# RWKV core of a four-layer backbone: triangular blocks of 16 instead of 32, joined by small TensorE products

## The chip, the cores and the metric

One Trainium2 chip, one of its cores. The metric is the device time of one execution in microseconds (us). Three runs of the kernel before took 2153.38 to 2157.12 us, median 2154.14 us. A fourth execution was profiled, and all rows below come from it.

## The reference, cut to what matters

Four layers (retention, mLSTM, RWKV-7, retention) over 256 context tokens and 256 latents of width 1024. Only the token mixing of layer 2 is touched. For each of 16 heads of width 64, in both directions, it runs

```
def step(S, inp):
    rt, wt, kt, vt, at, bt = inp
    sa = jnp.einsum('bhij,bhj->bhi', S, at)
    S = S * wt[:, :, None, :] + sa[..., None] * bt[:, :, None, :] + vt[..., None] * kt[:, :, None, :]
    return S, jnp.einsum('bhij,bhj->bhi', S, rt)
```

The term with `sa` makes each step depend on the one before. In a chunk of 64 steps it becomes a unit triangular matrix of 64 x 64 for each head, which has to be inverted before the chunk's outputs and its new state are plain matrix products.

## The kernel before

The core (`rk_core`) works in 8 batches, n = 0 to 7. Batch n holds chunks 2(n//2) and 2(n//2)+1 of both directions for one half of the heads (n%2): 4 units of 4 head pairs. The stages of a batch are

- P (`prep`, twice, one for each direction): loads, decay, scan on VectorE (L1294), the scaled operands W (L1301, L1308), bb (`bdA`, L1306) and kb (L1318, GpSimd).
- G (`grams1`, four times): 192-column products (L1328). Their triangles go to `AD` (four copies of 32 rows on ScalarE), the 32 x 32 part that lies off the diagonal goes to `off`, the rest to `RB`.
- H (`grams2`, four times): products for `AK` (L1344).
- I (`solve`): 32 x 32 triangles. `AD` is masked (L1366) and turned by a VectorE transpose in blocks of 32 into `LS` (L1367), so that each partition holds whole triangles. Then 30 steps run, each a product and an addition (L1378, L1379): the first 6 columns on GpSimd, in a copy that ScalarE makes, the others on VectorE. GpSimd's columns are copied back (L1381), the diagonal is set (L1382), and two transposes (L1384, L1385) give `O1` and `O2`.
- J (`whole`): two diagonal 32 x 32 blocks of each head and the block below become the 64 x 64 inverse `M`. Four ScalarE copies bring the diagonal blocks over, 16 products (L1396) make Q, which is copied, 16 products (L1403) make the lower block, which is copied. Then L1409 multiplies `M` by `RB`, which gives `G`.
- T (`step`, four times): L1424, L1426, L1433, L1435, L1436 and the state's update (L1439), with a state S for each direction and half.

ScalarE makes most copies, since `ENG[3]` sets `vcopy = copy`; `qcopy` and `gcopy` stay on VectorE.

Buffers tie the stages together. There are four W tiles, two in each batch, so P of batch n+2 writes what T of batch n read last. There is one `LS` and one `M`, two `AD`, and two PSUM banks under the tag `ps`, which whole, finish and others share.

The order written out is `ORDER`: in round n, P, G, H, I, J of batch n, and then T of batch n-1. What runs on an engine is not that order alone: the program is built with `schedule_with_timeline_sim=True`, and a planner lays each engine's instructions out by its own estimates. So instructions of other stages stand between the steps of a solve.

Batch 0 runs beside the last projections of the layer. The opening of the pools of the other batches (`second`) follows in the program behind them. Batch 7 is followed by `finish`, the output projection and the normalisation. Pieces of layer 3's modulation (`ada`, L308) are put beside batches 6 and 7.

Of the kernel before, what the change touches and what calls it, by code (L numbers as in the profile page):

```python
# [7 lines left out]
F32 = mybir.dt.float32  # L8
# [4 lines left out]
OP = mybir.AluOpType  # L13
# [18 lines left out]
SC = 6  # L32
# [100 lines left out]
class Net:  # L133
# [830 lines left out]
    def rwkv(self, i, j):  # L964
        nc, a = self.nc, self.a
        mm = nc.tensor.matmul
        with ExitStack() as es:
            prk = self.pool(es, "rk", 1)
            c = lambda name, *shape: prk.tile([128, *shape], F32, name=name)
            K = {}  # L970
            consts = (("mix", (6, 8)), ("kk", (8,)), ("hsel", (2,)), ("hb32", (128,)), ("w2", (1024,)), ("a2", (1024,)), ("ka", (8,)),
                      ("w0", (2, 8)), ("a0", (2, 8)), ("rk", (8,)), ("gng", (8,)), ("gnb", (8,)), ("II", (64,)), ("mak", (2, 128)),
                      ("mrb", (2, 64)), ("mtri", (32,)), ("reset", (512,)))
# [211 lines left out]
    def rk_core(self, es, e0, K, B, xd, h, xx, p1, p0):  # L1185
        nc = self.nc
# [57 lines left out]
        small = [t.rearrange("p (q h t) -> p q h t", q=4, h=2) for t in few[:8]]  # L1244
        roff = Ring(small, zero)
# [78 lines left out]
        def grams1(u, b0, AD):  # L1324
            d, W = u["d"], u["W"]
            g = two()
            for p in range(4):
                mm(g[:, p, 0:192], cat(u["bb"][:, p]), W[:, p], start=True, stop=True)  # L1328
            off = u["off"] = roff.next()
            for q in range(4):  # L1330
                r, half = slice(32 * q, 32 * q + 32), q % 2
                (vcopy if half else copy)(AD[r, :, b0:b0 + 4].rearrange("p t q -> p q t"), g[r, :, 32 * half:32 * half + 32])
            for h in range(2):
                r = slice(64 * h, 64 * h + 32)
                copy(off[r, :, h], g[r, :, 32:64])
# [25 lines left out]
        def solve(n, AD):  # L1361

            LS, O2 = [pool[tag] if tag in pool else pool.setdefault(tag, block(tag)) for tag in ("LS", "O2")]
            fl = lambda t: t.rearrange("p a b -> p (a b)")
            o = AD[:, :, 0:16]
            nc.vector.tensor_tensor(out=o, in0=o, in1=K["mtri"].unsqueeze(2).broadcast_to([128, 32, 16]), op=OP.mult)  # L1366
            nc.vector.transpose(fl(LS), fl(AD))  # L1367
            if SC:
                copy(fl(AD), fl(LS))
            for s in range(1, 31):  # L1370
                m = 31 - s

                for eng, A, lo, hi in ((nc.gpsimd, AD, 0, min(s, SC)), (nc.vector, LS, SC, s)):
                    if hi > lo:
                        n = hi - lo
                        t = p0.tile([128, SC * (31 - SC) if A is AD else (31 - SC) ** 2 // 4], F32, tag="sol" + "p" * (A is AD), bufs=1, name="sol")
                        t = t[:, 0:m * n].rearrange("p (a b) -> p a b", b=n)
                        eng.tensor_tensor(out=t, in0=A[:, s + 1:, s:s + 1].broadcast_to([128, m, n]), in1=A[:, s:s + 1, lo:hi].broadcast_to([128, m, n]), op=OP.mult)  # L1378
                        eng.tensor_tensor(out=A[:, s + 1:, lo:hi], in0=A[:, s + 1:, lo:hi], in1=t, op=OP.add)  # L1379
            if SC:  # L1380
                nc.gpsimd.tensor_copy(LS[:, :, 0:SC], AD[:, :, 0:SC])  # L1381
            nc.vector.memset(fl(LS)[:, ::33], 1.0)  # L1382
            O1 = AD
            nc.vector.transpose(fl(O1), fl(LS))  # L1384
            nc.vector.transpose(O2, LS.rearrange("p t s -> p s t"))  # L1385
            return O1, O2

        def whole(units, O1, O2):

            for q in range(4):  # L1390
                r, half = slice(32 * q, 32 * q + 32), q % 2
                (vcopy if half else copy)(M[r, :, q // 2, 32 * half:32 * half + 32], O2[r, :, 0:16].rearrange("p t q -> p q t"))
            Q = pool["Q"]
            qp = bank("ps").rearrange("p q t -> p (q t)")[0:64].rearrange("p (q t) -> p q t", q=16)
            for b in range(16):
                mm(qp[:, b], cat(units[b // 4]["off"][:, b % 4]), O2[:, :, b], start=True, stop=True)  # L1396
            for h in range(2):
                (qcopy if h else copy)(Q[64 * h + 32:64 * h + 64, :, h], qp[32 * h:32 * h + 32])
            for x in range(2):
                bs = slice(8 * x, 8 * x + 8)  # L1400
                tp = bank("ps").rearrange("p q t -> p (q t)")[0:32].rearrange("p (q h t) -> p q h t", q=8, h=2)
                for b in range(8):
                    mm(cat(tp[:, b]), O1[:, :, 8 * x + b], cat(Q[:, 8 * x + b]), start=True, stop=True)  # L1403
                for h in range(2):
                    (qcopy if h else copy)(M[64 * h + 32:64 * h + 64, bs, h, 0:32], tp[:, :, h])
# [142 lines left out]
        def second():  # L1548
# [4 lines left out]
            for nm in ("fin", "Y", "G", "mu", "rs", "bc"):  # L1553
                pool[nm] = p2
# [7 lines left out]
            pool["Q"] = p2.tile([128, 16, 2, 32], F32, name="Q")  # L1562
            zero(pool["Q"])
# [26 lines left out]
def host(inp):  # L1590
# [71 lines left out]
    a["rk_mtri"] = one(s % 32 < np.arange(32)[None, :])  # L1662
# [18 lines left out]
```

## Time and profile before

| what | value |
|---|---|
| median of 3 runs | 2154.14 us |
| profiled execution, time | 2151.38 us |
| its span, first to last instruction | 2149.6 us |
| core's batches, first transpose (L1367) of batch 0 to the last G copy of batch 7 | about 1225 to 1714 us of the span |
| mean granted TensorE clock | 0.957 |

A row of a timeline gives the start in us from the span's begin, the duration, the engine, line, operation, what is written and read, and how many instructions are merged. A float32 product shows as two records on PE and two on PEld. `ps`, `g` and `pp` are PSUM tiles, and some buffers go by the name of an earlier tile at their place: `bdB` is also `M`, `O` is `O2`, `q` and `lnsq` are `off`.

### The profile page before, as it was taken

How to read it: one execution, taken by the hardware profiler on the slowest of the kernel's cores; microseconds unless marked ns; L12 is line 12 of the kernel's file. 1: busy time of each engine (PE TensorE's matmuls, PEld its weight loads, DVE VectorE, ACT ScalarE, POOL GpSimd, SP SyncE). 2: the span in 40 equal slices, each digit the busy share in tenths (PEclk: the TensorE clock that was granted, in tenths of full speed). 3: DMA queues.
4: the chain of work that ended last, by engine and by line, in shares of the span. 5: the costliest groups of instructions: out<-in, count | busy, mean ns of one | idle time of the engine just before them, and what ended most of it. 6: DMA issues, size and time to landing. Idle time of an engine off the chain costs nothing. (4 is left out here: it accounts for less than half of the span.)

```text
span 2149.6 us, 35145 instructions
## 1 busy us (share of the span) xinstructions
PE 1947.1 (91%) x13562; PEld 1654.9 (77%) x13562; DVE 1344.2 (63%) x2456; ACT 941.9 (44%) x1851; POOL 612.7 (29%) x940
## 2 busy tenths in 40 slices
PE   7999999999999989989899987778778988999996
PEld 5788888877777777776658976677777776999995
DVE  4463635457646377576877467888776776665554
ACT  3242424233435454343445555556576352444433
POOL 1000000006200244322503257666555432311001
PEclk9999999999999989989899998999888999999998
DMA  9333324332545454343234411102123750233331
GB/s 303 109 108 114 122 90 134 106 108 75 196 168 178 148 174 153 112 130 109 99 115 161 150 55 54 35 23 66 32 74 94 224 173 1 79 118 118 118 103 46
DMA packets 241527, 245.94 MB, mean 114 GB/s; under 512 B 30992, under 2 KB 200080, under 8 KB 241360
## 3 DMA queue, kind: packets, MB, share of 16 engines
q1 hardware_dynamic: 241360, 243.70, 36.3%
q8 instruction: 107, 1.75, 0.3%
q14 instruction: 60, 0.49, 0.1%
HBM read 216.26 MB, written 27.39 MB: 113 GB/s over the span
## 5 line engine op out<-in xcount | busy, mean ns | idle before, releaser
L240 DVE TENSOR_TENSOR wl<-wraw,wh 128x1024 fp32r<-128x1024 f32 x216 | 270.5, 1254 | 192.1 <-ACT wh L238 187.3
L238 ACT ACTIVATE wh<-wraw 128x1024 fp32r<-128x1024 f32 x216 | 228.5, 1059 | 263.5 <-PE pp L257 119.3
L256 PE MATMUL pp<-hA,wh 128*128 128x512 f32 (+1 forms) x704 | 255.3, 365 | 7.1 <-DVE rp L527 3.0
L257 PE MATMUL pp<-hB,wh 128*128 128x512 f32 (+1 forms) x704 | 254.9, 363 | 0.0
L258 PE MATMUL pp<-hA,wl 128*128 128x512 f32 (+1 forms) x704 | 254.6, 363 | 0.1
L256 PE MATMUL pp<-zh,wh 128*128 128x512 f32 (+1 forms) x620 | 215.4, 350 | 10.1 <-ACT zh L288 6.0
L258 PE MATMUL pp<-zh,wl 128*128 128x512 f32 (+1 forms) x620 | 210.4, 340 | 0.0
L257 PE MATMUL pp<-zl,wh 128*128 128x256 f32 (+1 forms) x512 | 168.7, 330 | 3.0 <-DVE zl L289 3.0
L367 DVE SCALAR_TENSOR_TENSOR x<-pp,mod,x 128x256 f32<-128x256 f32 x192 | 87.3, 480 | 131.1 <-PE pp L258 130.8
L256 PEld LDWEIGHTS pp<-hA,wh 128*128 128x128 f32 x704 | 132.5, 189 | 32.0 <-PE pp L258 3.6
L258 PEld LDWEIGHTS pp<-hA,wl 128*128 128x128 f32 x704 | 133.1, 189 | 24.1 <-issue 1.6
L257 PEld LDWEIGHTS pp<-hB,wh 128*128 128x128 f32 x704 | 133.1, 189 | 22.4 <-issue 1.7
L256 PE MATMUL pp<-wh,hA 128*128 128x256 f32 x512 | 146.7, 288 | 2.0 <-ACT wh L238 1.9
L256 PEld LDWEIGHTS pp<-zh,wh 128*128 128x128 f32 x620 | 117.7, 191 | 37.9 <-issue 10.3
L257 PE MATMUL pp<-wl,hA 128*128 128x256 f32 x512 | 145.6, 285 | 0.5 <-DVE wl L240 0.5
L258 PE MATMUL pp<-wh,hB 128*128 128x256 f32 x512 | 145.3, 284 | 0.0
L258 PEld LDWEIGHTS pp<-zh,wl 128*128 128x128 f32 x620 | 117.8, 190 | 19.1 <-issue 6.7
L1378 POOL TENSOR_TENSOR sol<-AD 128x84 f32<-128x84 f32 (+13 forms) x240 | 94.7, 394 | 104.3 <-ACT AD L1198 86.5
L257 PEld LDWEIGHTS pp<-zl,wh 128*128 128x128 f32 x512 | 97.7, 191 | 16.7 <-issue 5.4
L1379 POOL TENSOR_TENSOR AD<-AD,sol 128x84 f32<-128x84 f32 (+13 forms) x240 | 101.8, 424 | 18.1
L256 PEld LDWEIGHTS pp<-wh,hA 128*128 128x128 f32 x512 | 97.7, 191 | 5.9 <-issue 2.6
L257 PEld LDWEIGHTS pp<-wl,hA 128*128 128x128 f32 x512 | 97.9, 191 | 1.4 <-DVE wl L240 0.8
(520 smaller groups left out, 4878.3 us busy)
## 6 DMA issues: line engine op xcount, KB each, us to landing
wraw<-ret_w_in SPq DMA_DIRECT2D x96, 512.0 KB, 3.7
wraw<-ada_w SPq DMA_DIRECT2D x56, 512.0 KB, 4.1
wraw<-ret_w_out SPq DMA_DIRECT2D x32, 512.0 KB, 3.4
wraw<-ml_w_in SPq DMA_DIRECT2D x32, 512.0 KB, 3.8
wraw<-rk_w_rkvg SPq DMA_DIRECT2D x32, 512.0 KB, 3.7
adaw<-ada_w SPq DMA_DIRECT2D x48, 256.0 KB, 4.6
raw<-ada_w SPq DMA_DIRECT2D x16, 512.0 KB, 7.8
wraw<-ml_w_out SPq DMA_DIRECT2D x16, 512.0 KB, 4.7
```

The costliest lines, as they stand in the source:

```text
L238: nc.scalar.activation(h, t, ACT.Copy)
L240: (nc.gpsimd if self.nsplit % 4 in self.psplit else nc.vector).tensor_tensor(out=l, in0=t, in1=f(h), op=OP.subtract)
L256: mm(ps, lhs[0], rhs[0], start=start, stop=False)
L257: mm(ps, lhs[0], rhs[1], start=False, stop=False)
L258: mm(ps, lhs[1], rhs[0], start=False, stop=stop)
L367: self.nc.vector.scalar_tensor_tensor(out=x, in0=ps, scalar=self.gate(i, c, st), in1=x, op0=OP.mult, op1=OP.add)
L1378: eng.tensor_tensor(out=t, in0=A[:, s + 1:, s:s + 1].broadcast_to([128, m, n]), in1=A[:, s:s + 1, lo:hi].broadcast_to([128, m, n]), op=OP. ...
L1379: eng.tensor_tensor(out=A[:, s + 1:, lo:hi], in0=A[:, s + 1:, lo:hi], in1=t, op=OP.add)
```

## The change

Blocks of 16 are inverted on VectorE alone: both diagonal 16 x 16 blocks of a triangle lie in one access pattern (`k`), 14 steps instead of 30. GpSimd has no part in the recursion. It cuts out the 16 x 16 blocks below the diagonal (`los`) first. Two rounds of 32 x 32 products, four at a time at the four diagonal positions of the array, join the blocks to inverses of 32 (`M`'s diagonal), a third gives their transposes (`MT`), and two rounds at two positions join 32 to 64.

```diff
-            LS, O2 = [pool[tag] if tag in pool else pool.setdefault(tag, block(tag)) for tag in ("LS", "O2")]
+            LS = p0.tile([128, 1056], F32, tag="LS", bufs=1, name="LS")
+            for b0 in (0, 8):
+                t = rLo.next()
+                nc.gpsimd.tensor_tensor(out=t, in0=AD[:, :, b0:b0 + 8], in1=K["m16"][:, 1].unsqueeze(2).broadcast_to([128, 32, 8]), op=OP.mult)
+                los.append(t)
             o = AD[:, :, 0:16]
-            nc.vector.transpose(fl(LS), fl(AD))
-            if SC:
-                copy(fl(AD), fl(LS))
-            for s in range(1, 31):
-                m = 31 - s
-                for eng, A, lo, hi in ((nc.gpsimd, AD, 0, min(s, SC)), (nc.vector, LS, SC, s)):
-                    ...
-            if SC:
-                nc.gpsimd.tensor_copy(LS[:, :, 0:SC], AD[:, :, 0:SC])
+            nc.vector.transpose(flat, fl(AD))
+            A = LS.rearrange("p (k x) -> p k x", x=528)[:, :, 0:512].rearrange("p k (a b) -> p k a b", b=32)
+            for s in range(1, 15):
+                m = 15 - s
+                t = p0.tile([128, 112], F32, tag="sol", bufs=1, name="sol")[:, 0:2 * m * s].rearrange("p (k a b) -> p k a b", k=2, b=s)
+                nc.vector.tensor_tensor(out=t, in0=A[:, :, s + 1:16, s:s + 1].broadcast_to([128, 2, m, s]), in1=A[:, :, s:s + 1, 0:s].broadcast_to([128, 2, m, s]), op=OP.mult)
+                nc.vector.tensor_tensor(out=A[:, :, s + 1:16, 0:s], in0=A[:, :, s + 1:16, 0:s], in1=t, op=OP.add)
...
+            ps, Pm = wide(), part("Pm")
             for b in range(16):
-                mm(qp[:, b], cat(units[b // 4]["off"][:, b % 4]), O2[:, :, b], start=True, stop=True)
...
+                for o, r in quarters:
+                    mm(ps[r, b], los[b // 8][r, :, b % 8], O2[r, :, b], start=True, stop=True, tile_position=(o, o))
+            nc.vector.tensor_tensor(out=Pm, in0=ps, in1=K["m16"][:, 2].unsqueeze(1).broadcast_to([128, 16, 32]), op=OP.add)
+            ps, MT = wide(), part("MT")
+            for b in range(16):
+                for o, r in quarters:
+                    mm(ps[r, b], O1[r, :, b], Pm[r, b], start=True, stop=True, tile_position=(o, o))
+            for q, (o, r) in enumerate(quarters):
+                (vcopy if q % 2 else copy)(M[r, :, q // 2, 32 * (q % 2):32 * (q % 2) + 32], ps[r])
+            ps = wide()
+            for b in range(16):
+                for o, r in quarters:
+                    mm(ps[r, b], Pm[r, b], O1[r, :, b], start=True, stop=True, tile_position=(o, o))
+            copy(MT, ps)
+            ps, Q = wide(), part("Pm")
...
+                    mm(ps[r2, b], units[b // 4]["off"][r, b % 4], M[r, b, h, 0:32], start=True, stop=True, tile_position=(o, o2))
+            for h, (o, r, o2, r2) in enumerate(low):
+                (qcopy if h else copy)(Q[r2], ps[r2])
...
+                    mm(ps[r2, b], MT[r2, b], Q[r2, b], start=True, stop=True, tile_position=(o2, o2))
+            for h, (o, r, o2, r2) in enumerate(low):
+                (qcopy if h else copy)(M[r2, :, h, 0:32], ps[r2])
```

Besides: `off` loses its zeroed half and takes half a small tile, `los` takes the other small tiles (`rLo`), the mask `mtri` becomes `m16` (three masks, 96 columns instead of 32), and the pool tile Q of 1024 columns goes for `Pm` and `MT` of 512 each.

## Rows read from the trace of the kernel before

**Rows 1.** The page, parts 1 and 2: busy shares, and tenths in 40 slices.
```profile
PE 1947.1 (91%) x13562; PEld 1654.9 (77%) x13562; DVE 1344.2 (63%) x2456; ACT 941.9 (44%) x1851; POOL 612.7 (29%) x940
...
POOL 1000000006200244322503257666555432311001
PEclk9999999999999989989899998999888999999998
```
**Rows 2.** Windows: busy us of each engine, clock, DMA; batch 0, 2 to 6, 7.
```profile
1224.00:1260.00 36.00, 36.00 (x180) 29.68 (x179) 30.64 (x62) 11.20 (x26) 24.24 (x61) 1.00 0.16 52
1345.00:1662.00 317.00, 251.10 (x2051) 228.63 (x2052) 247.36 (x496) 189.22 (x448) 190.96 (x372) 0.90 0.19 54
1662.00:1714.00 52.00, 47.98 (x634) 38.33 (x633) 38.28 (x101) 17.41 (x34) 23.45 (x66) 1.00 0.67 212
```
**Rows 3.** Groups by line, 1224 to 1714 us: count, busy us, mean ns, idle before.
```profile
L1379 POOL TENSOR_TENSOR AD<-AD,sol 128x84 f32<-128x84 f32 (+13 forms) x240 | 101.8, 424 | 18.1
L1378 POOL TENSOR_TENSOR sol<-AD 128x84 f32<-128x84 f32 (+13 forms) x240 | 94.7, 394 | 104.3 <-ACT AD L1198 86.5
L1379 DVE TENSOR_TENSOR LS<-LS,sol 128x24 f32<-128x24 f32 (+5 forms) x192 | 74.9, 390 | 6.7 <-ACT AD L1198 1.9
L1378 DVE TENSOR_TENSOR sol<-LS 128x24 f32<-128x24 f32 (+5 forms) x192 | 70.9, 369 | 4.7
...
L1358 DVE TENSOR_TENSOR AK<-g,cmak 128x512 f32<-128x512 f32 x32 | 21.7, 678 | 2.8 <-PE g L1344 1.5 <-ACT bon L1198 1.1
...
L1198 ACT ACTIVATE G<-ps 128x512 f32<-128x512 f32 x16 | 9.6, 601 | 9.4 <-PE ps L1409 9.4
```
**Rows 4.** Timeline: first and later links of the loop from batch 2 to 4.
```profile
1298.39 1.25 DVE L1367 STREAM_TRANSPOSE LS<-AD 128x1024 f32<-128x1024 f32 x1
...
1448.40 0.39 PE L1435 MATMUL pp<-S,W 128*128 128x128 f32 x2
...
1470.41 1.23 DVE L1367 STREAM_TRANSPOSE LS<-AD 128x1024 f32<-128x1024 f32 x1
...
1521.03 1.88 DVE L1385 STREAM_TRANSPOSE O<-LS 128x1024 f32<-128x1024 f32 x1
...
1539.93 2.05 PE L1409 MATMUL ps<-RB,bdB 128*128 128x128 f32 x16
...
1584.00 0.39 PE L1436 MATMUL pp<-bdB,G 128*128 128x128 f32 x2
```
**Rows 5.** Timeline of batch 7, from the solve's first transpose to L1409.
```profile
1663.17 1.24 DVE L1367 STREAM_TRANSPOSE LS<-AD 128x1024 f32<-128x1024 f32 x1
...
1697.02 1.92 DVE L1385 STREAM_TRANSPOSE O<-LS 128x1024 f32<-128x1024 f32 x1
...
1698.97 4.38 ACT L1198 ACTIVATE bdB<-O 32x512 f32<-32x512 f32 x4 [2.43 <-DVE O L1385]
...
1703.38 0.59 ACT L1198 ACTIVATE Q<-ps 32x512 f32<-32x512 f32 x1
...
1704.00 0.69 DVE L1199 COPY Q<-ps 32x512 f32<-32x512 f32 x1 [4.49 <-ACT Q L1198]
...
1704.83 1.94 PE L1403 MATMUL ps<-Q,AD 128*32 128x64 f32 x31 [0.95 <-DVE Q L1199]
...
1707.63 0.97 PEld L1409 LDWEIGHTS ps<-RB,bdB 128*128 128x128 f32 x8 [0.20 <-issue]
```
**Rows 6.** Groups by line and form, VectorE, 1428 to 1439 us.
```profile
L1378 DVE TENSOR_TENSOR sol<-LS 128x84 f32<-128x84 f32 x1 | 0.3, 319 | 0.0
...
L1379 DVE TENSOR_TENSOR LS<-LS,sol 128x84 f32<-128x84 f32 x1 | 0.2, 247 | 0.0
```
**Rows 7.** Groups by line and form, GpSimd, whole span.
```profile
L528 POOL TENSOR_TENSOR rp<-rp,rp 128x256 f32<-128x256 f32 x32 | 30.3, 948 | 194.7 <-DVE rp L527 194.6
```
**Rows 8.** Timeline, PE: four column tiles at once, and single products.
```profile
28.41 0.65 PE L308 MATMUL ps<-raw,csil 128*32 128x64 f32 x32 [0.64 <-DMA raw<-ada_w]
...
1698.99 1.13 PE L1396 MATMUL ps<-O,q 128*64 128x32 f32 x16 [1.31 <-DVE O L1385]
1699.95 1.11 PE L1396 MATMUL ps<-O,lnsq 128*64 128x32 f32 x16
```

More of the change, by code (lines that the diff above doesn't have):

```diff
@@ L31 @@
 ENG = (0, 0, 1, 1, 1, 0, 0, 0)
-SC = 6
 EARLY, FIN = 0, 3
@@ L1243, in rk_core @@
         zero(M)
-        small = [t.rearrange("p (q h t) -> p q h t", q=4, h=2) for t in few[:8]]
-        roff = Ring(small, zero)
+        roff = Ring([t[:, k:k + 128].rearrange("p (q t) -> p q t", q=4) for t in few[:4] for k in (0, 128)])
+        rLo = Ring([t.rearrange("p (t b) -> p t b", b=8) for t in few[4:8]])
         rW = Ring([p1.tile([128, 4, 2, 192], F32, tag=f"W{m}", bufs=1, name=f"W{m}") for m in range(2)], lambda t: nc.gpsimd.tensor_copy(
@@ L1334, in grams1 @@
                 r = slice(64 * h, 64 * h + 32)
-                copy(off[r, :, h], g[r, :, 32:64])
+                copy(off[r], g[r, :, 32:64])
             t = u["RB"] = rRB.next()
@@ L1361, in solve @@
         def solve(n, AD):
-            LS, O2 = [pool[tag] if tag in pool else pool.setdefault(tag, block(tag)) for tag in ("LS", "O2")]
+            LS = p0.tile([128, 1056], F32, tag="LS", bufs=1, name="LS")
+            O2 = pool["O2"] if "O2" in pool else pool.setdefault("O2", block("O2"))
             fl = lambda t: t.rearrange("p a b -> p (a b)")
-            o = AD[:, :, 0:16]
-            nc.vector.tensor_tensor(out=o, in0=o, in1=K["mtri"].unsqueeze(2).broadcast_to([128, 32, 16]), op=OP.mult)
@@ L1367, in solve @@
-            nc.vector.transpose(fl(LS), fl(AD))
-            if SC:
-                copy(fl(AD), fl(LS))
-            for s in range(1, 31):
-                m = 31 - s
-                for eng, A, lo, hi in ((nc.gpsimd, AD, 0, min(s, SC)), (nc.vector, LS, SC, s)):
[L1374 to L1379, printed above, removed]
@@ L1380, in solve @@
-            if SC:
-                nc.gpsimd.tensor_copy(LS[:, :, 0:SC], AD[:, :, 0:SC])
-            nc.vector.memset(fl(LS)[:, ::33], 1.0)
-            O1 = AD
[L1384 to L1394, printed above, removed]
-            for b in range(16):
-                mm(qp[:, b], cat(units[b // 4]["off"][:, b % 4]), O2[:, :, b], start=True, stop=True)
[L1397 to L1405, printed above, removed]
@@ new lines, in solve @@
+            for s in range(1, 15):
[3 more added lines that the diff above has]
+                nc.vector.tensor_tensor(out=A[:, :, s + 1:16, 0:s], in0=A[:, :, s + 1:16, 0:s], in1=t, op=OP.add)
+            nc.vector.memset(flat[:, ::33], 1.0)
@@ new lines, in solve, with whole @@
+            O1 = AD
+            nc.vector.transpose(fl(O1), flat)
+            nc.vector.transpose(O2, flat.rearrange("p (t s) -> p s t", t=32))
+            return O1, O2, los
+        def whole(units, O1, O2, los):
+            quarters = [(32 * q, slice(32 * q, 32 * q + 32)) for q in range(4)]
+            part = lambda name: tl(name, 1, 16, 32)
+            wide = lambda: bank("ps").rearrange("p q t -> p (q t)").rearrange("p (b t) -> p b t", t=32)
+            ps, Pm = wide(), part("Pm")
+            for b in range(16):
+                for o, r in quarters:
[13 more added lines that the diff above has]
+            ps, Q = wide(), part("Pm")
+            low = [(64 * h, slice(64 * h, 64 * h + 32), 64 * h + 32, slice(64 * h + 32, 64 * h + 64)) for h in range(2)]
+            for b in range(16):
+                for h, (o, r, o2, r2) in enumerate(low):
+                    mm(ps[r2, b], units[b // 4]["off"][r, b % 4], M[r, b, h, 0:32], start=True, stop=True, tile_position=(o, o2))
+            for h, (o, r, o2, r2) in enumerate(low):
+                (qcopy if h else copy)(Q[r2], ps[r2])
+            ps = wide()
+            for b in range(16):
+                for o, r, o2, r2 in low:
+                    mm(ps[r2, b], MT[r2, b], Q[r2, b], start=True, stop=True, tile_position=(o2, o2))
+            for h, (o, r, o2, r2) in enumerate(low):
+                (qcopy if h else copy)(M[r2, :, h, 0:32], ps[r2])
@@ L1552, in second @@
             p2 = self.pool(es, "c2", 1, side="right")
-            for nm in ("fin", "Y", "G", "mu", "rs", "bc"):
+            for nm in ("fin", "Y", "G", "mu", "rs", "bc", "Pm", "MT"):
                 pool[nm] = p2
@@ L1661, in host @@
     a["rk_mrb"] = c(one(np.stack([s <= t, 63 - s >= t], 1)))
-    a["rk_mtri"] = one(s % 32 < np.arange(32)[None, :])
+    s, t = (p % 32)[:, None], np.arange(32)[None, :]
+    a["rk_m16"] = c(one(np.stack([(s < t) & (s // 16 == t // 16), s // 16 < t // 16, s == t], 1)))
     r = np.ones((128, 512), np.float32)
```

7 lines of the change are left out of this document (4 added, 3 removed).

## The prediction

> **What bounds the kernel now.** I read the page first. PE is busy 91% of the span, yet in the slices of the RWKV core POOL's digit rises to 6 and the clock's falls to 8 [rows 1], so the core is another regime than the projections around it. The windows come next. In batches 2 to 6 PE is busy 251 of 317 us (79%) at a clock of 0.90, VectorE 247 (78%), POOL 191 (60%), ScalarE 189 (60%) [rows 2]: no engine is full, so latency and queues set the pace. The groups show who fills two engines: the recursion of solve, 480 instructions on POOL (196.5 us) and 384 on VectorE (145.8 us) [rows 3], that is 24.6 and 18.2 us in each of 8 batches. Last I read the timeline for the loop that sets the pace.
>
> The first transpose of the solve starts at 1298.39 us in batch 1 and at 1663.17 in batch 7 [rows 4, 5], 364.8 us for 6 batches: 60.8 us each. The loop reaches over two batches, because T of batch n frees the W tiles that P of batch n+2 writes. From batch 2 to 4 [rows 4]: last read of W at 1448.8, the transpose of batch 4's triangles at 1470.4 (21.6 us for P and G), the last transpose ends at 1522.9 (solve, 52.5), the first L1409 at 1539.9 (whole, 17.0), T ends at 1584.4 (44.5). The sum is 135.6 us for two batches. The largest link is the solve. Where little else is queued it takes 1663.17 to 1698.94, that is 35.8 us, and whole then takes 8.7 us, up to 1707.63 [rows 5]. The other 16.7 us of batch 4's solve are instructions of other stages that the planner put between its steps.
>
> **The change, part by part.** *Solve.* The POOL recursion goes, and with it the ScalarE copy and POOL's copy back. VectorE does 28 instructions instead of 48. Their sizes are 2s(15-s) for s = 1 to 14, 1120 elements in all, 80 on average. The nearest form is that of 84 elements: 319 and 247 ns at a time when few others ran [rows 6], mean 283. 28 x 0.283 = 7.9 us, and with 35 ns between two of them 8.9. The patterns have one dimension more, which no row shows: between 6 us (as the shortest quarter of the present ones) and 10.6 us (28 x 0.38, the present mean with POOL beside it [rows 3]); I keep 8.9. POOL's new part is two masks of 128 x 256. Such an instruction averages 0.95 us [rows 7]. The first reads units 0 and 1, which are there earlier, so one stands on the path, ahead of the VectorE mask that overwrites AD: +0.95. With the three transposes (1.24, about 1.25, 1.92 [rows 5]), the memset and hand-overs (0.3) the new solve takes 0.95 + 1.24 + 8.9 + 1.25 + 1.92 + 0.3 = 14.6 us instead of 35.8: -21.2 on the path.
>
> *Whole.* Two rounds of products become five: three of 64 (128 PE records each) and two of 32 (64 records). The price of a record is the unknown. Singly, 16 records of L1396 start within 0.96 us (1698.99 to 1699.95), 60 ns each, with a tail of 0.17 [rows 8]. Four column tiles at once: 32 records in 0.65 us, less that tail 15 ns each [rows 8]. No row has four row and column positions together. The ends are 7 ns (half as many columns as that row) and 60 ns. I take 15, the row that also runs four at a time, and 30 for the two-position rounds. That is 5 x 1.9 = 9.6 us of PE for each batch, where 64 x 60 ns = 3.8 go: +5.8.
>
> The Trainium skill has a rule against this: TensorE: Matmul & The Clock Gate, section "Wait — 56ns, not 53.3ns?", says that with one decode setting the sequencer spends about 62 ns on each matmul. By it 256 products would take 15.9 us, an estimate from that page, and the forecast would be some 35 us later. The row disagrees: 16 products (32 records) ran in 0.65 us, at most 41 ns each [rows 8].
>
> Between the rounds stand the addition that makes Pm (VectorE from PSUM, as AK, 0.68 [rows 3]), ScalarE's copies of M's diagonal (four at 0.59, the price of Q's copy [rows 5], three of which the next round needs, 1.8 us, covered by the third round), MT's copy (0.60, as G's [rows 3], covered by the fourth round), Q's copies and the last copies (0.69 each, ScalarE and VectorE side by side). The path is 9.6 + 0.68 + 0.69 + 0.69 + 6 hand-overs of 0.2 = 12.9 us instead of 8.7: +4.2. The four M copies of 4.38 us that read O2 strided [rows 5] go. ScalarE comes out lighter by some 2.5 us in a batch, which no path needs.
>
> *The rest has one answer.* A wider mask constant is loaded during the projections, small memsets go, `off` is half as large, and the pool tiles are as large as before: nothing, all of it ahead of batch 1 or on idle engines. SP gets no DMA more in the core.
>
> *What else moves.* VectorE per batch: 47.4 us now (247.4 x 60.8/317), minus 18.2 plus 7.9 plus 0.7: 38. POOL: 36.6 minus 24.6 plus 1.9: 14. PE: 48.2, of which at full clock some 43.4 would be left (x 0.90); plus 5.8 makes 49.2 us. So PE is late next: it sets a floor of about 49 us for a batch. New waits come on PE's queue: a round that waits for Pm or Q holds whatever is queued behind it, mostly products of T and G. Who waits for those is R's copies and the state's update.
>
> *Sum.* The loop over two batches: solve 52.5 becomes 14.6 plus as large a share of others' work as now (16.7 x 14.6/35.8 = 6.8), so -31; whole 17.0 becomes 12.9 plus five hops at about 2 us (two hops cost 8.3 beyond the 8.7 now; ScalarE and VectorE are less full), so +6. That is -25, or 48 us for a batch if only the loop counted. Loop and PE both lie near 49, and two limits so near each other cost beyond either; I take 53. Batches 1 to 7: 6 x (60.8 - 53) = 47. The tail from batch 7's solve: -21.2 + 4.2 = -17; DMA is at 0.67 and PE at 92% there with the next layer's modulation [rows 2], so I count half, -9. Batch 0: PE is full until the projections end (36.00 of 36.00 [rows 2]), its solve is covered, its longer whole is not: +4. Total -52: from the profiled execution's 2151.4 to 2099.5. The median lies 2.8 us above that execution: 2102.
>
> **The rivals.** *Deeper.* PE's tails overlap in the denser stream and the clock goes to full, T runs faster too: 47 us a batch, 6 x 13.8 = 83, the tail whole at 18: 2053. For it: PE's 48.2 includes time at half clock. Against: nothing has shown the core that dense.
>
> *Hops eat it.* Each of the five hops costs 4.1 us, as the two of batch 4 do (17.0 against 8.7), and the planner keeps 16.7 us of others' work inside the solve. Whole 33 (+16), solve 31 (-22): -6 for two batches, -18 in all, tail -5, batch 0 +4: 2135. For it: both are what batch 4 shows. Against: the queues get shorter.
>
> *Slower: the small tiles do not run together.* All products of a round write one PSUM bank from four row positions. If they went singly, 512 x 60 ns = 30.7 us in a batch, PE needs 43.4 - 3.8 + 30.7 = 70 us, above the present 60.8: 6 x 9.5 = +57, tail +3, batch 0 +15: 2229. It decides from 41 ns a record (43.4 - 3.8 + 512 x 0.041 = 60.8). The Trainium skill has this as a rule (TensorEngine Tiling (Array Packing), Restrictions and Gotchas, Gotcha 1): different row tiles cannot access one PSUM bank at the same time. No row here shows row tiles in one bank. Against it stands the 15 ns row, with column tiles alone in one bank.
>
> *No effect.* T or the planner's order holds the loop whatever the solve does: 2154.
>
> **How the numbers follow.** Forecast 0.48 (its own range 2080 to 2122), deeper 0.14, hops 0.21, singly 0.11, no effect 0.06. The range leaves out the singly and part of the deepest and the no-effect cases: 2046 to 2143. Faster by over 0.2% (4.3 us, about what a measurement of this kernel can tell from no change): forecast, deeper and nearly all of hops, 0.82; within 0.2%: 0.06; slower: singly and a little more, 0.12.
>
> **What would show it.** The recursion's 28 VectorE instructions near 0.28 us and a solve of 15 to 22 us from first to last transpose; the 64-product rounds at about 1.9 us, under 1 or near 8 would tell another price; transposes L1367's counterpart about 53 us apart; PE's windows over 90% busy with a clock above 0.90; POOL under 25% in the core. It would be wrong if whole takes over 30 us, if PE is still under 80% busy at a period near 60, or if the rounds go singly.

## The result

The changed kernel took 2124.29 us (median of 4 runs, 2119.65 to 2128.6), the kernel before 2153.76 in the runs beside it: a ratio of 0.9865, 95% interval 0.9849 to 0.988. The profiled execution took 2119.65 us with a span of 2117.9 (before 2151.38 and 2149.6), so 31.7 us less. That is within the forecast range, but the change is 32 us where 52 were forecast: batches 1 to 7 gave 8 more than forecast, batch 0 took 4 more, and the tail came out 24 us worse, against the forecast's sign. So the hit is in part luck, since two of the misses cancel in part.

The page of the changed kernel, parts 1 and 2, answers to [rows 1]:
```profile
PE 1968.9 (93%) x17146; PEld 1676.3 (79%) x17146; DVE 1260.9 (60%) x2296; ACT 919.6 (43%) x1841; POOL 430.5 (20%) x459
...
POOL 1000000004300143340700402332322033311001
PEclk9999999999999989999899998999999999999998
```
POOL loses 182 us, VectorE 83, and PE has 3584 records more. Windows of the same stretches as [rows 2]; columns are length, busy us of PE, PEld, VectorE, ScalarE and POOL, clock, DMA share, GB/s:
```profile
1224.00:1260.00 36.00, 36.00 (x180) 29.72 (x179) 18.84 (x42) 11.48 (x27) 0.63 (x1) 1.00 0.16 52
1345.00:1662.00 317.00, 296.45 (x5136) 267.57 (x5135) 216.85 (x455) 183.58 (x469) 79.45 (x80) 0.94 0.28 84
1662.00:1714.00 52.00, 46.85 (x400) 41.36 (x399) 32.59 (x60) 20.32 (x43) 3.72 (x3) 1.00 0.50 158
```
In the middle row PE goes from 251 of 317 us busy to 296 (94%): the core now waits for PE. The recursion, groups by line on VectorE from 1224 to 1714 us, answers to [rows 3, 6]:
```profile
L1378 DVE TENSOR_TENSOR sol<-LS 128x28 f32<-128x28 f32 (+6 forms) x112 | 27.9, 249 | 2.8
L1379 DVE TENSOR_TENSOR LS<-LS,sol 128x28 f32<-128x28 f32 (+6 forms) x112 | 27.0, 241 | 2.9
```
That is 28 instructions and 6.9 us a batch, for 18.2 on VectorE and 24.6 on POOL. Batch 4 in the timeline, from the first transpose of its solve to the first products with RB, answers to [rows 4, 8]. L1394, L1399 and L1405 are the rounds at four positions, L1411 and L1417 those at two, L1423 is the product with RB; the rows of T (L1447, L1450) are large products:
```profile
1453.38 1.23 DVE L1373 STREAM_TRANSPOSE LS<-AD 128x1024 f32<-128x1024 f32 x1
...
1474.33 2.23 PE L1394 MATMUL ps<-O,q 32*32 32x32 f32 x128 [1.00 <-DVE O L1383]
...
1478.31 0.64 PE L1450 MATMUL pp<-bdB,G 128*128 128x128 f32 x2
1478.74 0.64 PE L1447 MATMUL pp<-bdB,AK 128*128 128x128 f32 x2
...
1482.71 2.02 PE L1399 MATMUL ps<-Pm,AD 32*32 32x32 f32 x128
1484.56 1.63 PE L1405 MATMUL ps<-AD,Pm 32*32 32x32 f32 x99
1487.13 0.63 PE L1405 MATMUL ps<-AD,Pm 32*32 32x32 f32 x29 [0.94 <-issue]
...
1492.05 1.20 PE L1411 MATMUL ps<-bdB,q 32*32 32x32 f32 x64
...
1493.95 0.39 PE L1450 MATMUL pp<-bdB,G 128*128 128x128 f32 x2
1494.17 0.39 PE L1447 MATMUL pp<-bdB,AK 128*128 128x128 f32 x2
...
1497.69 1.19 PE L1417 MATMUL ps<-Pm,MT 32*32 32x32 f32 x62
...
1502.74 1.95 PE L1423 MATMUL ps<-RB,bdB 128*128 128x128 f32 x16
```
Three things stand here. Records start 14 to 16 ns apart at four positions (2.02 us for 128, with their tail) and 17 ns apart at two (1.19 us for 62). The third round breaks off after 99 records and stands idle for 0.94 us with "issue", that is, for nothing that the profile shows. And the products of T behind the first round start 0.43 us apart (1478.31 to 1478.74), where those at 1493.95 start 0.22 apart. Windows of the same kernel show why (the clock is the third number from the end):
```profile
1474.30:1476.50 2.20, 2.17 (x129) 2.15 (x129) 2.17 (x3) 0.58 (x3) 1.39 (x1) 1.00 0.03 7
1478.10:1481.50 3.40, 3.40 (x18) 3.18 (x17) 3.40 (x6) 2.49 (x8) 0.83 (x2) 0.51 0.02 5
1482.00:1488.00 6.00, 5.06 (x267) 4.64 (x265) 5.80 (x9) 3.56 (x6) 5.60 (x6) 1.00 0.40 113
1488.40:1491.80 3.40, 3.40 (x14) 3.28 (x12) 1.51 (x4) 3.06 (x6) 0.71 (x1) 0.50 0.62 188
```
Behind the first round, and again behind the second and third, the granted clock is at the lower of its two levels (0.50, 1.2 GHz), and the large products that follow pay for it.

**Where the time went.** Three pieces: batch 0's first transpose to batch 1's, 73.5 us before and 81.1 after (+7.6); batch 1's to batch 7's, 364.8 and 309.5 (-55.3; 51.6 us a batch for 60.8); batch 7's to the end of T of batch 7, 71.0 and 86.0 (+15.0). Together -32.7; the lead-in has 1.9 more, what follows 0.9 less. For this whole stretch the windows give, before and after:
```profile
1224.90:1734.20 509.30, 415.58 (x3454) 369.56 (x3452) 387.95 (x784) 285.27 (x671) 295.12 (x591) 0.91 0.26 77
```
```profile
1226.80:1703.40 476.60, 437.81 (x7037) 392.26 (x7035) 307.36 (x626) 263.53 (x664) 114.17 (x116) 0.93 0.28 84
```
The length splits into three terms. *Idle* is the length less PE's busy time. The trace also has the granted clock of each stretch. Large products at 0.50 start twice as far apart (0.43 us for 0.22 above), so half of the busy time that they spend there is lost to the *clock*. The rounds at two positions are counted with them (their records start 16.7 ns apart at 1.00 and 27 at 0.50). After, 43.9 us lie there, some 5 of them in these rounds, which makes 21.9. (The trace has 65 us at 0.50 in all; the rest of it is idle or rounds at four positions.) Products of the rounds at four positions start 14 ns apart at either level (L1405: 14.1 and 14.6 on average), so their time counts whole. All other busy time is *work*, in microseconds at full clock. The split holds where it can be tried: kernels with the same PE instructions have the same work (379.5 to 381.2 in before, e3, e5 and e8; 415.9 to 416.7 in the changed kernel, e1, e2 and e7), though their busy times differ by up to 34 and 14 us. In the rounds e4 and e11 issue other products, so there the work itself changes. The table has the kernels that change the core's products or waits.

| kernel | median us | stretch | work | clock | idle |
|---|---|---|---|---|---|
| before | 2153.8 | 509.3 | 381.2 | 34.4 | 93.7 |
| GpSimd out alone (e8) | 2168.2 | 520.8 | 381.2 | 45.0 | 94.6 |
| 14 steps alone (e5) | 2081.2 | 433.5 | 379.7 | 12.7 | 41.1 |
| changed kernel | 2124.3 | 476.6 | 415.9 | 21.9 | 38.8 |
| third round out (e9) | 2106.2 | 461.0 | 402.4 | 23.0 | 35.7 |
| the same, copies in another order (e10) | 2109.5 | 468.5 | 402.8 | 22.8 | 42.9 |
| third round and a wait out (e12) | 2114.0 | 468.3 | 403.2 | 29.7 | 35.4 |
| a wait out (e7) | 2144.8 | 503.0 | 416.7 | 35.1 | 51.2 |
| first round twice as wide (e11) | 2143.6 | 502.3 | 428.0 | 34.0 | 40.3 |
| first round twice (e6) | 2158.9 | 515.0 | 434.2 | 37.9 | 42.8 |
| one position at a time (e4) | 2232.5 | 585.0 | 531.1 | 42.6 | 11.3 |

The change takes 55 us of idle time and 12.5 of lost clock away and adds 35 us of work.

### The profile page after: what moved, and what is told of

Its sections match the earlier page's. It is cut to its first block, busy times and chain, and to the rows that moved or that the text cites. A ratio compares the mean times of both kernels' runs of the same rounds, so it can differ in the third digit from the quotient of the medians.

```text
span 2117.9 us, 41647 instructions
## 1 busy us (share of the span) xinstructions
PE 1968.9 (93%) x17146; PEld 1676.3 (79%) x17146; DVE 1260.9 (60%) x2296; ACT 919.6 (43%) x1841; POOL 430.5 (20%) x459
## 4 chain that ended last, share of the span: by engine, by line
PE 73%; DVE 12%; DMA 5%; ACT 5%; issue 3%; POOL 2%; SPq 0%; ACTq 0%; DVEq 0%; POOLq 0%
PE pp L255 15%; PE pp L256 15%; PE pp L257 15%; PE po L256 2%; PE ps L82 2%; PE g L1327 2%; PE po L257 2%; PE po L255 2%; PE ps L307 1%; DMA raw<-ada_w 1%; DVE wl L239 1%; PE g L1343 1%; PE pp L1450 1%; PE ps L255 1%; PE pp L1447 1%
## 5 line engine op out<-in xcount | busy, mean ns | idle before, releaser
L257 PEld LDWEIGHTS pp<-zh,wl 128*128 128x128 f32 x620 | 119.4, 193 | 19.3 <-issue 6.7
L257 PEld LDWEIGHTS pp<-wh,hB 128*128 128x128 f32 x512 | 97.5, 190 | 0.0
L288 DVE TENSOR_TENSOR vl<-pp,vh 128x256 fp32r<-128x256 f32 x64 | 26.9, 421 | 82.4 <-ACT vh L287 82.4
```

Source lines behind the costliest of these rows:

```text
L257: mm(ps, lhs[1], rhs[0], start=False, stop=stop)
L288: (eng or self.nc.vector).tensor_tensor(out=l, in0=src, in1=f(h), op=OP.subtract)
```

## The experiments

**The two halves of the change.** e5 has the new recursion and the old whole:
```diff
-            for s in range(1, 31):
-                m = 31 - s
+            A = LS.rearrange("p (k x) -> p k x", x=528)[:, :, 0:512].rearrange("p k (a b) -> p k a b", b=32)
+            for s in range(1, 15):
+                m = 15 - s
...
+                nc.vector.tensor_tensor(out=A[:, :, s + 1:16, 0:s], in0=A[:, :, s + 1:16, 0:s], in1=t, op=OP.add)
```


> The kernel before with the changed kernel's recursion alone: 14 steps on the two 16 x 16 blocks of each triangle, on VectorE, and the whole of before. It leaves out the joining of 16 to 32 (the blocks below the diagonal stay as they are), so it computes other numbers. It separates the short solve from the longer whole. Theory: the loop over two batches loses 37 us of 135.6 and PE needs 43 us of full clock a batch, so the period between first transposes of the solves is 47 to 50 us against 51.6 in the changed kernel and 60.8 before; the tail is longer as in the changed kernel: 2100 to 2112 us. Rival (PE alone sets the changed kernel's period): the period falls by the 5 us of PE that the new rounds add, to 46, and the time to 2090. Rival (the recursion was all there was to gain and whole costs nothing): 2124.

Measured: 2081.24 us (2080.79 to 2084.45), ratio 0.9666 (0.9641 to 0.9692), below the expected 2100 to 2112. The period of 49.3 us is the theory's; the tail is not longer, as the theory had it, but shorter, 66.2 us, and batch 0 to batch 1 takes 71.6. Its stretch:
```profile
1225.70:1659.20 433.50, 392.39 (x3455) 351.19 (x3454) 303.41 (x625) 278.48 (x666) 101.22 (x103) 0.96 0.31 91
```
So the short solve by itself is worth 73 us, and joining 16 to 32 gives 43 of them back: by the table, 36 of work and 9 of clock, less 2 of idle time.

e8 takes only GpSimd out:
```diff
-SC = 6
+SC = 0
```


> The kernel before with all 30 steps of the 32 x 32 recursion on VectorE (the first 6 columns too), GpSimd, the copy for it and the copy back left out, no joining by products at the level of 16. It parts the change in two: GpSimd out, and 14 steps for 30. VectorE: 60 instructions of 165 elements on average at 0.40 us or so, 24 us with gaps 26, and three transposes: a solve of about 30 us where little else is queued (35.8 with GpSimd). VectorE's load is 47.4 - 18.2 + 24 = 53 us for a batch of 60.8. Theory (the number of steps is what matters): a period of 57 to 60 and 2130 to 2152. Rival (the two engines delayed each other, GpSimd's exit is the gain): a period near 52 and 2110 or less.

Measured: 2168.21 us, ratio 1.0064 (1.0041 to 1.0088), slower, and above the expected 2130 to 2152. VectorE's recursion, all of it, and then one form of L1378 with 84 elements, in e8 and in the kernel before (groups by form, 1224 to 1740 and 1224 to 1714 us):
```profile
L1378 DVE TENSOR_TENSOR sol<-LS 128x30 f32<-128x30 f32 (+14 forms) x240 | 94.0, 392 | 5.8
L1379 DVE TENSOR_TENSOR LS<-LS,sol 128x30 f32<-128x30 f32 (+14 forms) x240 | 91.2, 380 | 5.8
```
```profile
L1378 DVE TENSOR_TENSOR sol<-LS 128x84 f32<-128x84 f32 x16 | 3.9, 245 | 0.4
```
```profile
L1378 DVE TENSOR_TENSOR sol<-LS 128x84 f32<-128x84 f32 x16 | 5.3, 334 | 0.4
```
At the same size the two engines did delay each other: 84 elements take 245 ns in e8, without GpSimd's recursion, and 334 in the kernel before, with it. But VectorE now does all columns, 165 elements on average in 60 instructions, and that is 23 us a batch for 18.2. With other stages' instructions between the steps the solve takes 57.7 us on average in batches 1 to 6, for 47.9 before. So GpSimd's exit gains nothing by itself; the gain needs fewer and smaller steps (e5).

**The price of a record.** e4 issues the 16 products of one position one after another in the four-position rounds:
```diff
-            for b in range(16):
-                for o, r in quarters:
+            for o, r in quarters:
+                for b in range(16):
```


> The changed kernel with the loops of the four-position and two-position rounds turned round where they were nested by quarter: the 16 products of one tile position follow one another, then the next position, so that neighbours in the queue use the same 32 x 32 tile. Same products, same bytes, same hops. Theory (the rounds are short because products at different positions run together): a record costs the 60 ns of 16 products on one place before, not 16 to 17, so a four-position round takes about 7.7 us instead of 2.1, three of them 23 instead of 6.3: +17 us of TensorE in each batch. It is at 94% of the period of 51.6 us already, so nearly all of it lengthens the period: 6 x 15 = +90, about 2215, and more if the batch before and the tail take their share (2230). Rival (a record costs what issuing it costs, wherever it goes): rounds of 2.1 us and 2124 within 5 us.

Measured: 2232.51 us, ratio 1.0363 (1.0336 to 1.0389), the upper of the theory's two numbers and nearly that of the prediction's rival "singly" (2229). A timeline of PE and windows of this kernel:
```profile
1333.44 7.67 PE L1394 MATMUL ps<-O,lnsq 32*32 32x32 f32 x128
...
1342.39 6.74 PE L1399 MATMUL ps<-Pm,AD 32*32 32x32 f32 x125
```
```profile
1228.60:1813.60 585.00, 573.66 (x7037) 526.64 (x7036) 301.98 (x626) 264.12 (x664) 107.81 (x116) 0.83 0.23 69
1335.70:1345.00 9.30, 9.30 (x146) 8.69 (x145) 5.25 (x7) 4.75 (x14) 4.45 (x4) 0.50 0.01 2
```
From start to start a record costs 52 to 58 ns, so it is the four positions that make it 14 to 16. In the stretch that is 115 us of work and 21 of clock, and 27 us of idle time are filled: 11 us of idle time are left. In the last row PE is busy for every one of 9.30 us, with small products one at a time, and is granted 0.50: here the lower clock does not come from an idle PE.

**What a round costs.** e6 issues the first round's products twice:
```diff
-                for o, r in quarters:
+                for o, r in 2 * quarters:
                     mm(ps[r, b], los[b // 8][r, :, b % 8], O2[r, :, b], start=True, stop=True, tile_position=(o, o))
```


> The changed kernel with every product of the first round (off-diagonal blocks of 16 by O2) issued twice into the same place: 128 records more, about 2.1 us of TensorE for each batch, no hand-over more. Theory (with blocks of 16 TensorE is what holds the batches, busy 296 of 317 us): the period grows by nearly all of it, 6 x 2 = +12, with +2 each between batches 0 and 1 and in the tail: about 2139. Rival (the hand-overs between rounds hold them, TensorE has 6% to spare): +2.1 us is taken from the waits of other stages, at most +4: 2128 or less.

Measured: 2158.93 us, ratio to before 1.0017 (1.0001 to 1.0034), so 35 us above the changed kernel, more than twice the theory's 15. Of 38.4 us in the stretch of the profiled execution 18.3 are work (2.3 a batch, as expected), 16.0 clock and 4.1 idle time: the clock nearly doubles the price. The doubled round in batch 4:
```profile
1500.13 4.13 PE L1394 MATMUL ps<-O,q 32*32 32x32 f32 x247 [0.49 <-DVE O L1383]
1505.16 0.34 PE L1394 MATMUL ps<-O,q 32*32 32x32 f32 x9 [0.91 <-issue]
```
It breaks off as well, after 247 records. The third part of the page names a cause: the queue whose packets are of the kind "instruction" moves (packets, MB, share) for before, the changed kernel and e6
```profile
q8 instruction: 107, 1.75, 0.3%
```
```profile
q8 instruction: 135, 2.21, 0.4%
```
```profile
q8 instruction: 143, 2.34, 0.5%
```
A packet is 16.4 KB, and 1024 records more are 8 packets more: 128 records each. So a round at four positions uses one packet up in 2.1 us, and in dense stretches the packets begin 3.3 to 4.3 us apart (here at 1502.80, 1506.52 and 1510.43 us). In the stretch, e6 has 18 breaks between two records of one round and the changed kernel 8; each of the 26 ends 1.23 to 1.51 us after such a packet has landed. The same holds for the 39 such breaks with "issue" of e7, e9, e10, e11 and e12 (1.08 to 1.56 us). So PE waits there for its next instructions. The Trainium skill (Runtime: NRT & Kernel Launch, section "Instruction fetch mechanics") says that crossing such a boundary is mostly hidden, since instructions are dispatched more slowly than they are fetched. These runs differ for records 14 to 16 ns apart; with e4's 52 to 58 ns no round breaks.

e11 makes the same round twice as wide with no more instructions:
```diff
-                    mm(ps[r, b], los[b // 8][r, :, b % 8], O2[r, :, b], start=True, stop=True, tile_position=(o, o))
+                    e = min(b + 2, 16)
+                    mm(ps[r, b:e], los[b // 8][r, :, b % 8], O2[r, :, b:e].rearrange("p t b -> p b t"), start=True, stop=True, tile_position=(o, o))
```


> The changed kernel with every product of the first round made twice as wide: the same weights, 64 columns of O2 for 32, so a product also writes the place of the next one, which that one overwrites. As much more streaming as in e6_first_round_twice (there 128 records more for a batch, 35 us more), but not one instruction more. Theory (what costs is the number of instructions in a dense train: a block of 16 KB of instructions, 128 records, arrives every 3.9 us at best where the rounds use one up in 2.1): 2124 within 6 us, the pauses inside rounds as in the changed kernel. Rival (what costs is the time that the array streams columns): a first round of 4 us or so and 2140 or more.

Measured: 2143.63 us, ratio to before 0.994 (0.9919 to 0.9962), 19 us above the changed kernel: the rival's number, and my theory fell (the packets also come 3.3 us apart at best, not 3.9). The round in batch 1, from a timeline of PE:
```profile
1321.14 3.75 PE L1395 MATMUL ps<-O,lnsq 32*32 32x64 f32 x128
```
Its records start 28 ns apart, so columns cost PE time even at four positions. In the stretch that is 12 us of work, 12 of clock, 1.5 of idle time; the breaks within rounds stay as many (9). So both count: columns as work, and instructions, of which e6 had more, as breaks. Clock is lost in both.

e7 takes the wait for Pm off the path:
```diff
-                    mm(ps[r, b], O1[r, :, b], Pm[r, b], start=True, stop=True, tile_position=(o, o))
+                    mm(ps[r, b], O1[r, :, b], O2[r, :, b], start=True, stop=True, tile_position=(o, o))
...
-                    mm(ps[r, b], Pm[r, b], O1[r, :, b], start=True, stop=True, tile_position=(o, o))
+                    mm(ps[r, b], O2[r, :, b], O1[r, :, b], start=True, stop=True, tile_position=(o, o))
```


> The changed kernel with the second and third round reading O2 in place of Pm, so neither waits for the first round or for the addition that makes Pm; both are still issued. Left out is what the first round contributes to the inverse. All of TensorE's products and all copies stay, one of the hand-overs on the path goes. Theory (TensorE's time holds the batches): -1 us or less a batch, 2115 to 2124. Rival (hand-overs hold them): the stretch from O2 to the first product with RB is 25 to 31 us for 8.4 us of rounds and four hand-overs on the path, some 4 us each beyond what the rounds take; one less is 6 x 2 to 4 = -12 to -24, about 2105.

Measured: 2144.76 us, ratio to before 0.9952 (0.9937 to 0.9967): 20 us slower than the changed kernel, against both expectations. Work is the same; clock costs 13 us more and idle time 12. Groups of PE over the stretch, of e7 and then of the changed kernel (after the second bar: idle time before them, and what ended it):
```profile
L1399 PE MATMUL ps<-O,AD 32*32 32x32 f32 x1024 | 18.4, 230 | 8.7 <-issue 8.6
L1405 PE MATMUL ps<-AD,O 32*32 32x32 f32 x1024 | 18.2, 235 | 13.0 <-issue 9.5 <-DVE Pm L1395 3.5
```
```profile
L1405 PE MATMUL ps<-AD,Pm 32*32 32x32 f32 x1024 | 18.1, 229 | 12.6 <-issue 12.6
L1399 PE MATMUL ps<-Pm,AD 32*32 32x32 f32 x1024 | 16.5, 222 | 1.2 <-issue 0.8 <-DVE Pm L1395 0.3
```
Without the wait the rounds stand in one train, that is, with nothing between them. In these two rounds "issue" is 18.1 us for 13.4, before all small products 24.5 for 14.0, and the clock is lower behind them. The way from O2 to the first product with RB did get shorter, 23.7 us for 27.0 on average in batches 1 to 6, and yet the period rose to 56.0 us. In the changed kernel the wait for Pm is where the planner puts T's large products. That this, and not an accident of the planner's order, made e7 slow had to be tried again (e12).

**The tail.** Layer 3's modulation (`ada`, 256 KB pieces) lies in it. e1 puts it behind T in the written order, e2 spreads it over earlier batches, e3 does the same in the kernel before:
```diff
-ORDER = "P0 P1 G0 G1 G2 G3 H0 H1 H2 H3 I0 J0 A0 T0-1 T1-1 T2-1 T3-1"
+ORDER = "P0 P1 G0 G1 G2 G3 H0 H1 H2 H3 I0 J0 T0-1 T1-1 T2-1 T3-1 A0"
```
```diff
-ADA3 = 0, 0, 0, 0, 0, 0, 1, 6
+ADA3 = 0, 0, 0, 1, 2, 3, 4, 6
```


> The changed kernel with one edit: in the order written out, the pieces of layer 3's modulation (stage A) come behind the four T of their round, not ahead of them. Theory: from 1630 to 1669 us the changed kernel's PE queue holds modulation products that wait for their weights (DMA at 0.72), and T of batch 6 and 7 stand behind them; so T of batch 7 ends 37 us behind the last G instead of 20 as before. With the pieces behind T the tail gives back 12 to 18 us: 2106 to 2112 us. Rival: T of the last batches is slow by itself (V loads, copies): within 4 us of the changed kernel's 2124.

> The changed kernel with the six modulation pieces spread over batches 3 to 7 (1, 1, 1, 1, 2) instead of 1 in batch 6 and 5 in batch 7. Theory of the tail: four of the five late pieces' loads leave the tail, where they took DMA at 0.72, and go to batches where DMA is at 0.23; they cost PE 1.7 us each there, where PE is at 94%. Tail -15, batches +5: 2112 to 2116 us. Rival (the tail does not hang on the modulation): 2124 to 2130.

> The kernel before with the same spreading of the modulation pieces. Theory: its tail was held by the solve and whole of batch 7 (1663 to 1714), beside which the modulation loads ran, so little changes: 2148 to 2156 us. Rival (the modulation held the tail of both kernels alike): 2136 to 2142, and then the longer tail of the changed kernel has another cause.

Measured: e1 2122.93 us (ratio to before 0.9859, 0.9835 to 0.9884), e2 2124.36 (0.9863, 0.9838 to 0.9888), e3 2153.78 (0.9999, 0.9985 to 1.0013). None moves the time by more than these runs can tell, so the theories of e1 and e2 fell and that of e3 held. But e2 does shorten the tail, from 86.0 to 71.5 us (7.5 us of that are work), and the batches ahead of it take 54.9 us each for 51.6: what leaves the tail comes back in the period. Over the whole stretch e2 has the work and the idle time of the changed kernel (416.6 and 38.9). So where the modulation stands decides how long the tail is, and not how long the kernel is.

**A version with one round less.** e9 makes MT by a VectorE transpose:
```diff
-            ps = wide()
-            for b in range(16):
-                for o, r in quarters:
-                    mm(ps[r, b], Pm[r, b], O1[r, :, b], start=True, stop=True, tile_position=(o, o))
-            copy(MT, ps)
+            nc.vector.transpose(fl(MT), fl(ps))
```


> The changed kernel without its third round: the transposes MT of the inverses of 32 come from one VectorE transpose of the second round's PSUM in blocks of 32 (128x512, half of L1373's size) instead of 64 products and ScalarE's copy. Theory (each round of small products costs TensorE its own length, the pause in its instruction supply and a stretch at the lower clock behind it): the third round is 2.0 us long and 1.1 us stands idle inside it in each batch, 8 x 3.1 = 25, and doubling the first round cost 35 us although its own length is 2.1 us a batch; so -25 to -35: 2090 to 2099. Rival (the planner's order of the whole batch decides, since leaving out a hand-over alone moved the time by +20): no relation to the records taken out, 2110 to 2145.

Measured: 2106.18 us (2105.26 to 2106.92), ratio to before 0.9773 (0.9758 to 0.9787), 18 us under the changed kernel and better than both kernels. The direction is the theory's, the size half to three quarters of it: work -13.5, idle -3.1, clock +1.1. The round's own length came back nearly whole (8 x 2.0 = 16). The "issue" idle time before small products fell from 14.0 to 1.0 us, yet idle time as a whole by 3: other waits took its place. And e9 did not get back what e6 had paid in clock: a round more cost 16 us of it, a round less saved none.

e10 adds another order of M's copies:
```diff
-            for q, (o, r) in enumerate(quarters):
-                (vcopy if q % 2 else copy)(M[r, :, q // 2, 32 * (q % 2):32 * (q % 2) + 32], ps[r])
+            for q in (0, 2, 1, 3):
+                o, r = quarters[q]
+                (qcopy if q == 2 else copy)(M[r, :, q // 2, 32 * (q % 2):32 * (q % 2) + 32], ps[r])
```


> The kernel of e9_mt_by_transpose with M's diagonal copied in another order: the two quarters that the next round reads first, one on ScalarE and one on VectorE, then the two that only the products with RB read. On the path of each batch two ScalarE copies of 0.59 us fewer stand ahead of the fourth round. Theory (TensorE's time holds the batches): as e9_mt_by_transpose within 4 us. Rival (hand-overs hold them): 8 x 1.2 = -10.

Measured: 2109.53 us (2104.46 to 2110.8), ratio to before 0.9781 (0.976 to 0.9801): 3 us above e9, within the theory's 4 us, and no difference that these runs can tell. In the profiled execution the stretch is 7.5 us longer than e9's, nearly all of it idle time.

e12 repeats e7's edit on e9 (the first of its two lines; the other went with the third round). 

> The kernel of e9_mt_by_transpose with the second round reading O2 in place of Pm, so that it waits neither for the first round nor for the addition; both are still issued. Left out is what the first round contributes to the inverse. It repeats e7_no_pm_hop (which was 20 us slower than the changed kernel, although a wait was gone) on the version with four rounds. Theory (without the wait the rounds stand closer together, 128 products in one train: TensorE then pauses for instructions within it and its clock falls behind it): against e9_mt_by_transpose more pauses within rounds (4 of 3.4 us in all there), more busy time at the lower clock (46 us there, between batch 0's transposes and the end of T of batch 7), and 5 to 20 us more, 2111 to 2126. Rival (e7's loss was an accident of the planner's order; a wait less is a gain): 2106 or less.

Measured: 2113.95 us (2110.17 to 2116.54), ratio to before 0.9813 (0.9787 to 0.9839), 8 us above e9. L1400, the second round, of e9 and then of e12, groups of PE over the stretch:
```profile
L1400 PE MATMUL ps<-Pm,AD 32*32 32x32 f32 x1024 | 16.7, 217 | 1.4 <-issue 1.0 <-DVE Pm L1396 0.3
```
```profile
L1400 PE MATMUL ps<-O,AD 32*32 32x32 f32 x1024 | 18.8, 229 | 11.0 <-issue 11.0
```
The breaks come back, the busy time at 0.50 rises from 45.9 to 65.2 us, and the clock's term of the table by 6.7 us, while work and idle time stay within 1. So e7's sign repeats, and so does its share in clock: the wait between two rounds was filled with large products, and taking it away costs clock and saves no waiting. How much of e7's 20 us is the planner's order remains open.

## Why the prediction was right, and where not

*Solve: right.* Forecast 14.6 us, of which 0.95 was the mask ahead of the first transpose; from that transpose on batch 1's takes 14.6, and batches 1 to 6 average 17.6 for 47.9 before: -30.3, forecast -31. The recursion is 6.9 us for 7.9, since an instruction costs 245 ns on average and not 283 (the row of the forecast stood beside GpSimd's recursion, see e8); POOL's mask is 0.63 for 0.95.

*Price of the rounds: right.* Five rounds take about 8.9 us in the rows of batch 4, forecast 9.6. The row with four column tiles [rows 8] was the right one to go by, and e4 shows that it hung on the positions: 15 ns was forecast, 14 to 16 came, and one position at a time it would have been 52 to 58. At two positions it is 17, not 30. The Trainium skill's Gotcha 1 (TensorEngine Tiling (Array Packing), Restrictions and Gotchas), that different row tiles cannot access one PSUM bank at the same time, is not borne out: four row positions wrote one bank with records 14 to 16 ns apart. Nor do the 62 ns for each matmul show here that the Trainium skill gives for one decode setting (TensorE: Matmul & The Clock Gate, "Wait — 56ns, not 53.3ns?"): 64 products in 2.02 us are 32 ns each.

*Whole: +11, forecast +6.* From O2 to the first product with RB batches 1 to 6 take 27.0 us on average, 16.0 before. The rounds are shorter than forecast, so the hand-overs (a copy on another engine between two rounds, and the wait for PE behind it) cost more: batch 4's rows have T's products between the rounds, some of them at half clock. The sign of being wrong, a whole of over 30 us, came in batch 3 (30.8) and in batch 0 (49.9, 21.5 before), not on average. With the solve this is -19.3 for the loop over two batches, 9.7 a batch; the period fell by 9.2.

*Period: 51.6, forecast 53, by terms that traded places.* I put PE's floor at 49.2 us a batch and 4 on top. Between batch 1's and batch 7's transposes PE's work is 46.1 us a batch (42.2 before: +3.9, not +5.8), clock costs 2.6 and idle time 2.9. So the floor was 3 us lower, and what I called the price of two near limits was half of it clock, which my sum had let rise to full. Nothing in [rows 2], where a clock of 0.90 stood beside a PE that was 79% busy, said that it would. One step of the sum is also off: the 25 us were read from a loop of 135.6 us, but taken off twice the average period (121.6). By the loop's own length 55 a batch would have come, not 48; 53 lay between them.

*Tail: +15, forecast -9.* This is the step that failed. It was written as "-21.2 + 4.2 = -17; DMA is at 0.67 and PE at 92% there with the next layer's modulation [rows 2], so I count half, -9". The solve did shorten by 18.3 us. But PE was busy 64.7 of the tail's 71.0 us before, so at most 6 could be had with this work in it, whatever the solve's length; the half had no row. e5, with the short solve alone, had 4.9. Against the tail before, the changed kernel's has 5.8 us more work, 2.9 more clock and 6.3 more idle time. How much of that work is the rounds' and how much was pushed there from earlier batches is open (e2 moved 7.5 us of it out). Timeline of batch 7 in the changed kernel, answering to [rows 5]:
```profile
1617.37 1.25 DVE L1373 STREAM_TRANSPOSE LS<-AD 128x1024 f32<-128x1024 f32 x1
...
1632.91 1.92 DVE L1383 STREAM_TRANSPOSE O<-LS 128x1024 f32<-128x1024 f32 x1
...
1641.88 1.95 PE L1399 MATMUL ps<-Pm,AD 32*32 32x32 f32 x122 [0.83 <-issue]
...
1647.00 2.02 PE L1405 MATMUL ps<-AD,Pm 32*32 32x32 f32 x123 [3.10 <-issue]
...
1660.56 2.05 PE L1423 MATMUL ps<-RB,bdB 128*128 128x128 f32 x16
```
From O2 (1634.8) to L1423 it takes 25.7 us where [rows 5] had 8.7: two breaks of 0.83 and 3.10 us lie in it (each behind the first five records of its round), and the modulation's products stand between the rounds.

*Batch 0: +7.6, forecast +4.* The longer whole is on the path, as said: 5.4 us are work, 1.4 clock, 0.8 idle. e5, without the rounds, has none of it (71.6 us for 73.5).

*The rivals.* "Deeper" had the order of its period (47), which only e5 came near (49.3). "Hops eat it" (2135) was right that the hand-overs are dearer, but e7 and e12 show that taking one away gains nothing, and e10 that shortening one gains nothing. "Singly" is e4's kernel, 2232.5 for 2229, but the parts differ: its period is 66.6 us for 70, and its tail is 25 us longer for 3, so that the totals meet is luck. "No effect" is out.

## What to carry over

Where a change fills idle time of one engine with its work, split each stretch into work at full clock, lost clock and idle time before costing it. What does not take work away can only save the other two, and a stretch in which PE is already 91% busy at full clock has next to none of them. Small products at four tile positions are cheap one by one, but a longer train of them can cost twice its own length (e6), mostly through the clock behind it: leave out rounds (e9) rather than waits (e7, e12), and let large products stand between two rounds.

## What the runs showed of the hardware

- Records of 32 x 32 float32 products start 52 to 58 ns apart on average at one position, 14 to 16 at four, and 28 at four with 64 columns, the narrow ones alike at either clock (L1405: 14.1 and 14.6 ns; e4's L1394: 58.6 and 57.9). At two positions it is 16.7 ns at 1.00 and 27 at 0.50.
- TensorE's granted clock fell to 0.50 in or behind rounds of small products in all 11 of the changed kernel's low stretches of the core, and in e4 while PE was busy without a break. The kernel before, whose PE is idle for 93.7 of 509.3 us, has 17 low stretches there without one such product, so such rounds are not needed for it. Most of the changed kernel's rounds have breaks or waits of PE beside them, and no run tells which of the two lowers the clock there. Large products at 0.50 start 0.43 us apart for 0.22.
- PE's instructions come in packets of 16.4 KB, 128 records here. In dense trains the packets begin 3.3 to 4.3 us apart, and PE stands still until 1.2 to 1.5 us after one has landed. That is seen in 26 of 26 breaks inside rounds of the changed kernel and e6, and within 1.1 to 1.6 us in 39 more of other kernels; why the next packet is not asked for earlier no run here shows.
- A VectorE instruction of the recursion on 84 elements takes 334 ns on average where GpSimd has a part in the recursion (before) and 245 where it has none (e8).
